# A new opening for a hybrid encoder block: 512-column value products, w_ada rows summed on VectorE, 4 KB loads

## The chip, the core and the metric

The kernel runs on one core of one Trainium2 chip. The metric is the device time of one execution in microseconds (us). The engines are TensorE (PE, matmuls; PEld is its weight load), VectorE (DVE), ScalarE (ACT), GpSimd (POOL) and SyncE (SP), which here issues nearly all DMAs. SBUF is the on-chip memory, PSUM the eight banks into which PE writes, HBM the main memory.

## The reference, cut to what matters

The block takes x (1024 positions by 1024 features, float32) and a conditioning vector c. Its opening is:

```python
ada = jax.nn.silu(c) @ w_ada[i] + b_ada[i]                 # 1024 -> 6 x 1024
shift1, scale1, gate1, shift2, scale2, gate2 = [...]       # ada in six parts
h = rmsnorm(x, g_mix[i]) * (1 + scale1) + shift1
proj = h @ w_in[i]
qa, ka, va, qb, kb, vb, ga, gb = jnp.split(proj, split_at, axis=-1)
oa = mixture_of_dilations(heads(qa), heads(ka), heads(va), rel_bias)
ob = neighbourhood_attention_2d(heads(qb), heads(kb), heads(vb), na_rpb[i])
```

va and vb have 512 columns each: 8 heads of 64 for branch A (dilated window attention) and for branch B (neighbourhood attention). After it come the two attentions, the gated merge with w_out, and a convolutional feed-forward layer with w_up and w_down. All of that stays as it is.

## The kernel before, in words

Every float32 operand of a large product is split into a high part (float32r, made by ACT) and the remainder (DVE or POOL: `split`, lines 54 to 56), and a product is three matmuls: high by high, high by low, low by high (`product`, lines 72 to 79). x lies in HBM as eight blocks k of 128 features by 1024 positions. The positions are worked in two halves of 512.

The opening is lines 110 to 369, most of it inside a block in which the order of every engine is written out by hand (`tc.manual_schedule`, line 288). It does this:

- It loads the first half of x in eight DMAs of 256 KB (`x_load`, 2 KB per partition), the first two chunks of w_ada, and halves of four weight tiles of w_in: q and k of head pair 0, and 256 columns of va.
- `square` (line 182) squares x on ACT and adds the squares on DVE; `square_sums`, `rstd_of` and `bcast` make the norm's factor in all partitions (PE sums, DVE, ACT, PE transposes).
- The w_ada chunks 0 to 3 hold shift1 and scale1, each for two of the eight blocks k. A chunk has eight rows of [128, 512]; each row is weighted with one column of silu(c) and all are added. In these four chunks three or four of the rows are weighted on ACT and added on POOL (`ada_rows_pool`, line 159), three or four on DVE (`ada_rows`, line 150, lines 155 and 157 of the profile), DVE joins the two (`ada_join`), and PE sums over the partitions (`ada_sums`, line 141). `piece_bias` (lines 263 and 265) then has the shift and scale of two blocks k.
- x is multiplied with the norm's factor on DVE or POOL (`scale_x`, line 206), and `modulate` (lines 212 to 215) makes the high and low part of h: ACT makes the high part from x, DVE the full value from x, DVE or POOL the difference.
- In four steps, each with two blocks k, PE then does the products of q and k of pair 0 with the first half (lines 77 to 79) and of 256 columns of va for four tiles of 128 positions (lines 247 to 249).
- Then the other 256 columns of va, the second half of x, and from line 484 on, left to a scheduler, the rest: query and key of pair 0 for the second half, va for the second half, vb in two halves of 256 columns, with w_ada chunks 4 to 11 (`ada_chunk`, line 168) in between. `va_chunks` and `vb_chunks` copy the values in HBM into the arrangements that the attentions read.

A chunk of w_ada is four DMAs of 512 KB, into tiles of several pools. Then comes `attend_dil` for pair 0: bias tables and values are loaded (lines 529 to 531, 449 to 452, `v_tile` at 473), the scores S (lines 557 and 558) go to a softmax (541, 542). Later pairs' query and key products and the gate products fill PE between the attention's matmuls.

Of the kernel before, what the change touches and what calls it, by code (L numbers as in the profile page):

```python
# [28 lines left out]
def hybrid_encoder(tc, xT, c, w_ada, small, w_in, p1_bias, p23_bias, na_bias, ln2_mult, ident, w_br, w_out,  # L29
# [55 lines left out]
    ps_g = tc.alloc_tile_pool(name="psg", bufs=2, space=PSUM)  # L85
    qkpool = tc.alloc_tile_pool(name="qk", bufs=3)
# [23 lines left out]
    early = tc.alloc_tile_pool(name="early", bufs=1, reuse_waits="tile")  # L110
    adapool = tc.alloc_tile_pool(name="ada", bufs=1, reuse_waits="tile")
    work = tc.alloc_tile_pool(name="start", bufs=2, reuse_waits="tile")
    ps_n = tc.alloc_tile_pool(name="psn", bufs=1, space=PSUM, reuse_waits="tile")
    ps_s = tc.alloc_tile_pool(name="psst", bufs=1, space=PSUM, reuse_waits="tile")

    slots = iter(range(1 << 20))

    def wada_tile(j):
        n = next(slots) if j < 4 else -1
        if n == 0:  # L120
            return qkpool.tile([128, 2, 512], FT, name="kl")
        if n > 0 and (n - 1) % 6 < 2:
            return early.tile([128, 2, 512], FT, name="wada", bufs=2)
        return adapool.tile([128, 2, 512], FT, name="wada", bufs=4)

    def ada_load(j):

        rows = []
        for t in range(0, KT, 2):
            wt = wada_tile(j)  # L130
            sp.dma_start(wt, w_ada[j][:, t:t + 2])
            rows += [wt[:, i] for i in range(2)]
        return rows

    def ada_sums(parts, pa=None, stop=True, n=4):

        first = pa is None
        pa = ps_s.tile([128, 4], FT, name="pada", bufs=1) if first else pa
        for i, (w, col) in enumerate(parts):
            for m in range(n):  # L140
                pe.matmul(pa[:, m:m + 1], w[:, m * 128:(m + 1) * 128], col, start=first and i + m == 0,
                          stop=stop and i == len(parts) - 1 and m == n - 1, skip_group_check=True)
        return pa

    def ada_bias(c0, pa, n=4):

        cc = slice(c0, c0 + n)
        dve.tensor_tensor(ada[:, cc], pa[:, :n], b_ada[:, cc], OP.add)

    def ada_rows(wt, ts, acc=None):  # L150

        for t in ts:
            if acc is None:
                acc = wt[t]
                dve.tensor_scalar(acc, acc, cs[:, t:t + 1], None, OP.mult)
            else:
                dve.scalar_tensor_tensor(acc, wt[t], cs[:, t:t + 1], acc, OP.mult, OP.add)  # L157

    def ada_rows_pool(wt, ts):
        for t in ts:  # L160
            act.activation(wt[t], wt[t], AF.Copy, scale=cs[:, t:t + 1])
        for t in ts[1:]:
            pool.tensor_tensor(wt[ts[0]], wt[ts[0]], wt[t], OP.add)

    def ada_join(wt, a, b):
        dve.tensor_tensor(wt[a], wt[a], wt[b], OP.add)

    def ada_chunk(j, wt):
        ada_rows(wt, range(KT))
        ada_bias(4 * j, ada_sums([(wt[0], ones)]))  # L170

    def x_load(hf, ks=range(KT)):
        x = []
        for k in ks:
            x.append(early.tile([128, 512], FT, name="xl", bufs=1) if hf + k == KT else h_tile(FT))
            sp.dma_start(x[-1], xT[k][:, halves[hf]])
        return x

    def sq_accs():
        return [early.tile([128, 512], FT, name="sq", bufs=2) for _ in range(2)]  # L180

    def square(x, accs, ks, e):
        for k in ks:
            acc = accs[k // 4]
            sq = early.tile([128, 512], FT, name="mt", bufs=4) if k % 4 else acc
            act.activation(sq, x[k], AF.Square)
            if k % 4:
                e.tensor_tensor(acc, acc, sq, OP.add)

    def square_sums(accs):  # L190
        pcol = ps_n.tile([128, KT], FT, name="pcol")
        add_sums(pcol, accs[0], True, False)
        add_sums(pcol, accs[1], False, True)
        return pcol

    def norm_bcast(pcol):
        return bcast(rstd_of(pcol, 4), ps_n, "pbc")

    def to_sbuf(pb):
        bc = early.tile([128, 512], FT, name="mt", bufs=4)  # L200
        act.activation(bc, pb, AF.Copy)
        return bc

    def scale_x(x, pb, bc, ks, e):
        for k in ks:
            e.tensor_tensor(x[k], x[k], pb if e is dve else bc, OP.mult)

    def modulate(x, hf, ks, lo_eng):
        for k in ks:
            a, b = am1[:, k:k + 1], ada[:, k:k + 1]  # L210
            hi, lo = h[hf, k] = h_tile(), h_tile()
            act.activation(hi, x[k], AF.Identity, bias=b, scale=a)
            t = early.tile([128, 512], FT, name="mt", bufs=4)
            dve.tensor_scalar(t, x[k], a, b, OP.mult, OP.add)
            lo_eng[k % 2].tensor_tensor(lo, t, f(hi), OP.subtract)  # L215

    def v_load(br, hv):
        return [w_load(w_in[(8, 20)[br] + 2 * hv + t]) for t in range(2)]

    v_pools = itertools.cycle((early, work))  # L220

    def v_tiles():
        p = next(v_pools)
        return tuple(p.tile([128, KT, 256], FR, name=n, bufs=1) for n in ("vwh", "vwl"))

    def v_split(raws, lo_eng, ks=slice(0, KT), w=None):
        hi, lo = w or v_tiles()
        for t in range(2):
            cc = slice(t * 128, t * 128 + 128)
            split(raws[t][:, ks], hi[:, ks, cc], lo[:, ks, cc], lo_eng[t])  # L230
        return hi, lo
# [8 lines left out]
    def v_product(st, w, p=None, ks=range(KT), fresh=True):  # L240

        hi, lo = w
        p = ps_s.tile([128, 512], FT, name="pv", bufs=3)[:, :256] if p is None else p
        sc = slice(st % 4 * 128, st % 4 * 128 + 128)
        for k in ks:
            hhi, hlo = (t[:, sc] for t in h[st // 4, k])
            pe.matmul(p, hhi, hi[:, k], start=fresh and k == 0, stop=False, skip_group_check=True)  # L247
            pe.matmul(p, hhi, lo[:, k], start=False, stop=False, skip_group_check=True)  # L248
            pe.matmul(p, hlo, hi[:, k], start=False, stop=k == KT - 1, skip_group_check=True)  # L249
        return p  # L250

    def v_out(br, hv, st, p):
        vs = work.tile([128, 256], FT, name="vs", bufs=3)
        act.activation(vs, p, AF.Copy)
        sp.dma_start((va_s, vb_c)[br][st * 128:st * 128 + 128, hv * 256:hv * 256 + 256], vs)
# [32 lines left out]
    with tc.manual_schedule(engines={e.engine for e in (sp, act, dve, pool, pe)}):  # L288
# [64 lines left out]
        for st in range(4):  # L353
            v_out(0, 0, st, pvs[0][st])
# [1007 lines left out]
```

## Time and profile before

| | |
|---|---|
| median of 3 runs | 1631.35 us (1630.24 to 4495.99) |
| profiled execution | 1631.86 us |
| its span in the profile | 1630.1 us |
| mean granted PE clock | 0.976 |
| PE busy | 1511.3 us (93%), 7884 matmuls |
| DVE / ACT / POOL busy | 1125.0 / 784.3 / 795.8 us |
| DMA | 196.87 MB, mean 121 GB/s |

The profile is of one execution. A row of a timeline has start and duration in us, engine, line, operation, out<-in, shape, how many in a row, and in brackets the idle time before it and what ended it. A row of stretches has the stretch, then busy us (and count) for PE, PEld, DVE, ACT and POOL, the granted PE clock, the busy share of the 16 DMA engines and GB/s. Starts of successive matmuls tell their pace better than their durations, since matmuls overlap.

### The profile page before, as it was taken

To read this page: it belongs to the slowest core of one execution; us is meant where nothing else is said; L and a number is where in the kernel's file an instruction comes from. 1 tells how busy PE (TensorE), PEld (TensorE's weight loads), DVE (VectorE), ACT (ScalarE), POOL (GpSimd) and SP (SyncE) were. 2 spreads that over 40 slices of the span, in tenths; PEclk is the share of its full clock that TensorE was granted. 3 is DMA by queue.
4 is the path that set the end of the run, shared out by engine and by line. 5 is a ranking of instruction groups with operands and counts; after the bars stand their busy time and mean duration, and the time that the engine had idled before them with its cause. 6 is when DMAs were issued, how large, how long until landed. Compare 5 with 4: busy or idle time off the path is not lost. (4 is left out here: it accounts for less than half of the span.)

```text
span 1630.1 us, 21921 instructions
## 1 busy us (share of the span) xinstructions
PE 1511.3 (93%) x7884; PEld 1285.9 (79%) x7884; DVE 1125.0 (69%) x1902; ACT 784.3 (48%) x1408; POOL 795.8 (49%) x493
## 2 busy tenths in 40 slices
PE   4898899999998999999999898999999997888998
PEld 3898888888897987887778677888888885766787
DVE  6886476676767766535625898876666669798875
ACT  4531276665766766543335454444444444333232
POOL 4442133243224443311156777676666666868622
PEclk9898999999999999999999999999999999999999
DMA  6749812222233452555534122232222232513222
GB/s 232 256 157 318 257 51 89 70 82 88 61 99 99 127 143 88 170 182 173 169 129 159 61 73 83 78 116 78 78 78 78 78 136 81 190 39 126 91 61 104
DMA packets 113525, 196.87 MB, mean 121 GB/s; under 512 B 40328, under 2 KB 61704, under 8 KB 113416
## 3 DMA queue, kind: packets, MB, share of 16 engines
q1 hardware_dynamic: 113144, 195.20, 36.6%
q8 instruction: 62, 1.02, 0.3%
q14 instruction: 47, 0.39, 0.1%
q10 hardware_dynamic: 272, 0.26, 0.0%
HBM read 158.73 MB, written 42.47 MB: 123 GB/s over the span
## 5 line engine op out<-in xcount | busy, mean ns | idle before, releaser
L56 POOL TENSOR_TENSOR wlo<-wraw,whi 128x1024 fp32r<-128x1024 f32 (+2 forms) x77 | 179.3, 2328 | 308.0 <-ACT whi L55 289.1
L77 PE MATMUL pj<-h,whi 128*128 128x512 f32 x448 | 181.8, 407 | 17.5 <-DVE kl L429 9.8
L78 PE MATMUL pj<-h,whi 128*128 128x512 f32 x448 | 180.2, 402 | 1.2 <-DVE h L215 1.2
L79 PE MATMUL pj<-h,wlo 128*128 128x512 f32 x448 | 179.8, 401 | 0.0
L56 POOL TENSOR_TENSOR wsl<-big,wsh 128x1024 fp32r<-128x1024 f32 (+1 forms) x45 | 110.2, 2451 | 61.6 <-ACT wsh L55 61.6
L1049 DVE SCALAR_TENSOR_TENSOR big<-wc,sm,big 128x256 f32<-128x256 f32 (+1 forms) x132 | 115.3, 921 | 17.2 <-ACT big L1043 17.2
L55 ACT ACTIVATE whi<-wraw 128x1024 fp32r<-128x1024 f32 (+2 forms) x81 | 81.0, 1000 | 77.2 <-PE pj L78 34.1
L77 PEld LDWEIGHTS pj<-h,whi 128*128 128x128 f32 x448 | 85.7, 192 | 35.6 <-issue 7.0
L78 PEld LDWEIGHTS pj<-h,whi 128*128 128x128 f32 x448 | 86.0, 192 | 16.8 <-DVE h L215 2.3
L79 PEld LDWEIGHTS pj<-h,wlo 128*128 128x128 f32 x448 | 85.7, 191 | 15.5
L542 ACT ACTIVATE P<-P,st 128x256 f32<-128x256 f32 x128 | 64.3, 503 | 47.2 <-DVE st L541 46.6
L541 DVE CUSTOM_DVE_ANT_0 P<-S,bias 128x256 f32<-128x256 f32 x128 | 52.1, 421 | 46.8 <-PE S L588 35.3
L474 POOL TENSOR_TENSOR vv<-vv 96x256 fp32r<-96x256 f32 (+2 forms) x32 | 40.9, 1287 | 85.3 <-ACT vv L473 62.5
L157 DVE SCALAR_TENSOR_TENSOR wada<-wada,cs 128x512 f32<-128x512 f32 x67 | 65.7, 980 | 19.4 <-DMA wada<-w_ada 17.6
L1049 DVE SCALAR_TENSOR_TENSOR big<-pj,sm,big 128x512 f32<-128x512 f32 x132 | 67.9, 563 | 16.1 <-ACT big L1043 16.1
L694 POOL TENSOR_SCALAR P<-P,stb 128x288 f32<-128x288 f32 (+1 forms) x32 | 40.2, 1257 | 79.1 <-DVE stb L691 62.1
L429 DVE SCALAR_TENSOR_TENSOR kl<-pj,ks 64x512 fp32r<-64x512 f32 x64 | 56.3, 880 | 30.3 <-ACT ks L427 29.7
L247 PE MATMUL pv<-vwh,h 128*128 128x256 f32 x256 | 74.4, 291 | 0.0
L56 POOL TENSOR_TENSOR wsl<-wraw,wsh 128x768 fp32r<-128x768 f32 (+1 forms) x23 | 53.4, 2323 | 42.9 <-ACT wsh L55 42.9
L249 PE MATMUL pv<-vwh,h 128*128 128x256 f32 x256 | 74.0, 289 | 0.0
L1043 ACT ACTIVATE big<-wc,sm 128x512 f32<-128x512 f32 x44 | 35.8, 815 | 79.0 <-DVE wc L877 45.8
L248 PE MATMUL pv<-vwl,h 128*128 128x256 f32 x256 | 73.4, 288 | 0.0
(360 smaller groups left out, 4948.4 us busy)
## 6 DMA issues: line engine op xcount, KB each, us to landing
wada<-w_ada SPq DMA_DIRECT2D x47, 512.0 KB, 5.3
wraw<-w_in SPq DMA_DIRECT2D x36, 512.0 KB, 4.0
big<-w_up SPq DMA_DIRECT2D x22, 512.0 KB, 5.5
wraw<-w_up SPq DMA_DIRECT2D x22, 512.0 KB, 3.6
as<-big SPq DMA_DIRECT2D x22, 512.0 KB, 3.0
big<-as SPq DMA_DIRECT2D x22, 512.0 KB, 7.7
wraw<-w_down SPq DMA_DIRECT2D x24, 384.0 KB, 3.6
gs<-gs SPq DMA_DIRECT2D x32, 256.0 KB, 2.0
```

The source lines that it names most:

```text
L55: act.activation(hi, raw, AF.Copy)
L56: lo_eng.tensor_tensor(lo, raw, f(hi), OP.subtract)
L77: pe.matmul(psum, whi[:, k0 + k], mhi, start=k == 0, stop=False)
L78: pe.matmul(psum, whi[:, k0 + k], mlo, start=False, stop=False)
L79: pe.matmul(psum, wlo[:, k0 + k], mhi, start=False, stop=k == n - 1)
L157: dve.scalar_tensor_tensor(acc, wt[t], cs[:, t:t + 1], acc, OP.mult, OP.add)
L247: pe.matmul(p, hhi, hi[:, k], start=fresh and k == 0, stop=False, skip_group_check=True)
L248: pe.matmul(p, hhi, lo[:, k], start=False, stop=False, skip_group_check=True)
L249: pe.matmul(p, hlo, hi[:, k], start=False, stop=k == KT - 1, skip_group_check=True)
L429: dve.scalar_tensor_tensor(ll[x], pp[a], 0.125, f(kh[a]), OP.mult, OP.subtract)
L542: act.activation(pp, pp, AF.Exp, bias=mi, scale=-1.0, accum_out=li)
L1049: dve.scalar_tensor_tensor(y[:, dst], src, wt, y[:, dst], OP.mult, OP.add)
```

## The change

The opening is written anew. Outside of it, two things change: `qk_tiles` no longer takes products begun in the opening, and x, whose layout in HBM is now [half][four pairs of k][128][2][512], is read back in the later stage with another index (256 KB as before).

- **Loads.** x comes in four DMAs of 512 KB for each half (4 KB per partition). The value weights have an array of their own, `w_v` [2][4][128][2][512], and are loaded as pairs of k for all 512 columns of a branch, 512 KB each. Neither q and k nor half tiles are loaded at the start.
- **w_ada.** All rows are added on DVE (`ada_rows`), into a small tile; of chunks 0 to 3, rows 6 and 7 are summed by PE directly with a column of silu(c). ACT and POOL have no part in it. The chunks go into whole 16 KB tiles (`t0`, `b1`, `b2`) that later or earlier hold split value weights, or into the four tiles of x: from chunk 4 on they alternate between `t0` and the x tiles.
- **modulate** takes x, scale and the norm's factor in one DVE instruction into a PSUM bank, ACT adds the shift and makes the high part from there, and DVE makes the low part from both. `scale_x` is gone.
- **Order.** PE does the values alone, 512 columns wide: branch A on the first half in four steps of two k, then 24 steps n of one k each: B on the first half, A on the second, B on the second. Between them stand the sums of w_ada chunks 4 to 11, one every second n. Query and key of pair 0 come behind all of it; their weights are split at n = 12. DVE splits no weights any more, POOL splits all.
- **Memory.** One PSUM pool of eight banks (five for values, two for stages, one for norms) is released before the query/key pool is made.

The core of the diff:

```diff
+    def ada_rows(rows, ts, acc=None):
+        for t in ts:
+            if acc is None:
+                acc = small_tile()
+                dve.tensor_scalar(acc, rows[t], cs[:, t:t + 1], None, OP.mult)
+            else:
+                dve.scalar_tensor_tensor(acc, rows[t], cs[:, t:t + 1], acc, OP.mult, OP.add)
+        return acc
...
+    def modulate(x, hf, ks, pb):
+        for k in ks:
+            hi, lo = h[hf, k] = h_tile(), h_tile()
+            t, b = stage(), ada[:, k:k + 1]
+            dve.scalar_tensor_tensor(t, x[k], am1[:, k:k + 1], pb, OP.mult, OP.mult)
+            act.activation(hi, t, AF.Identity, bias=b)
+            dve.scalar_tensor_tensor(lo, t, b, f(hi), OP.add, OP.subtract)
...
+    def v_split(raw, w, kp):
+        for i in range(2):
+            split(raw[:, i], w[0][:, 2 * kp + i], w[1][:, 2 * kp + i], pool)
+
+    def v_products(w, hf, k, banks, ts=range(4)):
+        hi, lo = w
+        for t in ts:
+            p = banks[t]
+            hhi, hlo = (x[:, t * 128:t * 128 + 128] for x in h[hf, k])
+            pe.matmul(p, hhi, hi[:, k], start=k == 0, stop=False, skip_group_check=True)
+            pe.matmul(p, hhi, lo[:, k], start=False, stop=False, skip_group_check=True)
+            pe.matmul(p, hlo, hi[:, k], start=False, stop=k == KT - 1, skip_group_check=True)
...
+        rows = {0: ada_load(0, "t0")}
+        raws = [v_load(0, 0)]
+        rows[1] = ada_load(1, "b1")
+        raws.append(v_load(0, 1))
+        rows[2] = ada_load(2, "b2")
+        raws += [v_load(0, kp) for kp in (2, 3)]
+        rows[3] = ada_load(3, "t0")
+        x.append(x_load(1))
+        vw = [(t16("a0"), t16("a1"))]
+        pcol = norm_sums(squares(x[0], (dve, dve)))
+        acc = ada_rows(rows[0], range(4))
+        r = rstd_of(pcol, 4)
+        pb = bcast(r, ps, "pc")
+        acc = ada_rows(rows[0], (4, 5), acc)
+        pa = ada_sums([(rows[0][t], cs[:, t:t + 1]) for t in (6, 7)] + [(acc, ones)])
+        v_split(raws[0], vw[0], 0)
+        banks = v_banks()
+        for q in range(4):
+            piece_bias(q, pa)
+            modulate(x[0], 0, range(2 * q, 2 * q + 2), pb)
+            v_products(vw[0], 0, 2 * q, banks)
             if q < 3:
+                v_split(raws[q + 1], vw[0], q + 1)
+                acc = ada_rows(rows[q + 1], range(6))
+                pa = ada_sums([(rows[q + 1][t], cs[:, t:t + 1]) for t in (6, 7)], stop=False)
+            v_products(vw[0], 0, 2 * q + 1, banks, (0, 1))
+            if q < 3:
+                ada_sums([(acc, ones)], pa)
+            v_products(vw[0], 0, 2 * q + 1, banks, (2, 3))
+        raws = [v_load(1, kp) for kp in range(4)]
+        vw.append((t16("b1"), t16("b2")))
+        rows = {4: ada_load(4, "t0"), 5: ada_load(5, None)}
+        pcol = norm_sums(squares(x[1], (dve, pool)))
+        v_split(raws[0], vw[1], 0)
+        r = rstd_of(pcol, 4)
+        v_split(raws[1], vw[1], 1)
...
+        for n in range(24):
+            g, k = divmod(n, 8)
+            br, hf = ((1, 0), (0, 1), (1, 1))[g]
+            if k == 0:
+                v_out(*old)
+                banks = v_banks()
+                old = br, hf, banks
+            if n == 17:
+                va_chunks(slice(0, 512))
+            v_products(vw[br], hf, k, banks)
+            if n == 1:
+                pb = bcast(r, ps, "pc")
+                modulate(x[1], 1, range(8), pb)
+            if n in (0, 1):
+                v_split(raws[n + 2], vw[1], n + 2)
+            if n in (5, 6):
+                qk_raw.append(w_load(w_in[4 * (n - 5)]))
+            i = n // 2 - 2
+            if n % 2 == 0 and i >= 0:
+                if i >= 2:
+                    pa = ada_sums([(accs[i - 2], ones)])
+                if i < 8:
+                    accs[i] = ada_rows(rows[4 + i], range(KT))
+                if i >= 2:
+                    ada_bias(4 * (i + 2), pa)
+                if i < 6:
+                    rows[6 + i] = ada_load(6 + i, (None, "t0")[i % 2 == 0])
+            if n == 12:
+                qk_w = [w_split(qk_raw[i], pool) for i in range(2)]
+        v_out(*old)
...
-        "xT": x[0][_POS].T.reshape(KT, 128, S),
+        "xT": x[0][_POS].T.reshape(4, 2, 128, 2, 512).transpose(3, 0, 2, 1, 4),
```

More of the change, by code (lines that the diff above doesn't have):

```diff
@@ L108, in h_tile @@
         return hpool.tile([128, 512], dtype, name="h", bufs=32)
[L110 to L143, printed above, removed]
@@ L217, in v_load @@
[L217 to L231, printed above, removed]
+    xpool = tc.alloc_tile_pool(name="xs", bufs=4, side="right", reuse_waits="tile")
```

296 lines of the change are left out of this document (97 added, 199 removed).

## The prediction, made before the changed kernel had run

> **What bounds the kernel now.** I read the profile page first, then the stretches of the first 230 us, then the timelines of TensorE (PE), VectorE (DVE), ScalarE (ACT), GpSimd (POOL) and SyncE (SP) there, and the order of instructions of both builds.
>
> ```profile
> span 1630.1 us, 21921 instructions
> PE   4898899999998999999999898999999997888998
> DMA  6749812222233452555534122232222232513222
> PE 32%; DVE 8%; issue 2%; DMA 0%; POOL 0%; ACT 0%; SPq 0%; DVEq 0%; ACTq 0%; POOLq 0%
> 0.00:230.00 230.00, 190.36 (x1260) 176.36 (x1261) 161.06 (x242) 95.90 (x182) 83.18 (x58) 0.94 0.66 221
> 300.00:1630.00 1330.00, 1251.49 (x6221) 1049.01 (x6219) 916.59 (x1523) 642.55 (x1115) 687.27 (x417) 0.98 0.33 106
> 140.00:180.00 40.00, 40.00 (x343) 40.00 (x341) 23.11 (x31) 6.43 (x15) 4.80 (x2) 1.00 0.96 319
> ```
>
> PE is busy 94% after 300 us, but 83% in the first 230 (the last two numbers of a stretch are the DMA share and GB/s). The change lies in that opening. (The chain that ended last does not reach back to it: it explains 42% of the span, from the end.) Behind it the two builds issue the same matmuls, from the second half of the attention on in the same order, so what the opening gains or loses is passed on to the end one for one. As landmark I take the restart of the attention scores, with all value products and the first 144 query/key products done:
>
> ```profile
> 27.63 0.79 PE L77 MATMUL pj<-h,whi 128*128 128x512 f32 x1 [3.83 <-ACT h L212]
> 29.80 0.63 PE L78 MATMUL pj<-h,whi 128*128 128x512 f32 x1
> 30.22 0.63 PE L79 MATMUL pj<-h,wlo 128*128 128x512 f32 x1
> 101.62 0.28 PE L247 MATMUL pv<-vwh,h 128*128 128x256 f32 x1
> 101.74 0.28 PE L248 MATMUL pv<-vwl,h 128*128 128x256 f32 x1
> 101.86 0.95 PE L141 MATMUL pada<-ones,wada 128*128 128x1 f32 x8
> 130.13 1.84 PE L141 MATMUL pada<-ones,wada 128*128 128x1 f32 x8 [7.08 <-issue]
> 193.25 0.39 PE L78 MATMUL pj<-h,whi 128*128 128x512 f32 x1
> 193.48 0.40 PE L79 MATMUL pj<-h,wlo 128*128 128x512 f32 x1
> 198.67 0.58 PE L557 MATMUL S<-ks,qs 128*128 128x256 f32 x1 [4.79 <-DVE st L541]
> ```
>
> From start to start: a 512-column matmul takes 0.23 us, 0.43 after an idle stretch; a 256-column one 0.12. A four-column w_ada sum (x8) takes 0.95, cold 1.84. By 198.67 PE has done 768 x 0.12 + 144 x 0.23 = 125 us of products; some 15 us are sums, and the rest is waiting and cold clock.
>
> **The change, part by part.**
>
> *Fewer, wider matmuls.* 768 x 0.12 = 92.2 become 384 x 0.23 = 88.3 us: -3.9 us of PE work, contained in the times below. They come in four groups of 96: branch A and branch B on the first half of x, then A and B on the second; a group has eight k, each of 12 matmuls (2.77 us). The query/key products stay 144, but none is interleaved with the value products any more.
>
> *The start.* Rows for this and the next part:
>
> ```profile
> 4.00:6.00 2.00, 0.00 (x0) 0.00 (x0) 0.00 (x0) 0.98 (x2) 0.00 (x0) 1.00 0.76 253
> 12.00:14.00 2.00, 1.05 (x6) 0.97 (x6) 0.95 (x2) 1.41 (x2) 0.00 (x0) 1.00 1.03 418
> L186 ACT ACTIVATE mt<-h x11: 615/629/630, 5.6 to 68.9; 128x512 f32<-128x512 f32 x11
> 15.68 1.12 PE L104 MATMUL pbc<-idt,rs 128*128 128x128 f32 x4 [0.71 <-DVE rs L98]
> 12.36 0.69 DVE L188 TENSOR_TENSOR sq<-sq,mt 128x512 f32<-128x512 f32 x1
> 26.38 0.15 DVE L263 TENSOR_TENSOR ada<-pada,sm 128x4 f32<-128x4 f32 x1
> 63.60 0.17 DVE L263 TENSOR_TENSOR ada<-pada,sm 128x4 f32<-128x4 f32 x1 [1.90 <-PE pada L141]
> 26.76 1.52 ACT L212 ACTIVATE h<-h,ada,am 128x512 fp32r<-128x512 f32 x2 [6.29 <-DVE am L265]
> 57.98 1.54 DVE L157 SCALAR_TENSOR_TENSOR wada<-wada,cs 128x512 f32<-128x512 f32 x2
> 29.98 6.72 DVE L157 SCALAR_TENSOR_TENSOR wada<-wada,cs 128x512 f32<-128x512 f32 x4
> 29.58 3.21 POOL L163 TENSOR_TENSOR wada<-wada 128x512 f32<-128x512 f32 x2 [3.68 <-ACT wada L161]
> 101.29 1.38 DVE L429 SCALAR_TENSOR_TENSOR kl<-pj,ks 64x512 fp32r<-64x512 f32 x2
> 17.83 1.31 ACT L55 ACTIVATE whi<-wraw 128x512 fp32r<-128x512 f32 x2
> ```
>
> x comes in four 512 KB loads instead of eight of 256 KB; the queue moves 253 GB/s at 4 to 6 us and 418 at 12 to 14, when 512 KB pieces of w_ada are in it, so I give it 0.9 us: the last square add ends at 12.1, not 13.05. Then DVE adds four w_ada rows (0.5 + 3 x 0.77) to 15.0, norm 0.6 and broadcast 1.1 to 16.8; PE's sums of rows 6 and 7 and of the accumulator are 24 cold matmuls instead of 16, at 1.84 per 8: 22.3. So the first bias (L263) stands at 22.2 instead of 26.38.
>
> *The four steps of the first half.* One step, from bias to bias: bias 0.4; then modulate, which now runs through PSUM as a chain, DVE 0.69, ACT 0.65, DVE 0.69 with three 0.05 us hand-overs, 2.1 us for each k and 4.2 for two (before, ACT and DVE both started from x: L212 0.72 each); then six rows on DVE, 0.5 + 5 x 0.77 = 4.4 us; then the sum 1.0. That is 10.0 us. POOL runs two weight splits of about 1.6 us under the rows, and the rows show what that does: four DVE adds took 6.72 us beside POOL, 1.7 each, against 0.77 alone. So 3.2 us of POOL costs DVE 1.7: 11.7 us for a step. [...] Three steps end at 22.2 + 35.1 = 57.3 (before: 63.60). PE needs some 8 us for a step and hides. The last 24 matmuls start 1.75 us later and take 5.5: 64.6.
>
> *From group to group.* PE now waits for x's second half: ACT's squares follow its last modulate (57.3 + 3.8 = 61.1) and take 8 x 0.63, POOL adds three of them behind (about 1.4 each) to 69.3, PE sums 1.0, and the first weight split of branch B ends at 70.7, on the same POOL queue. So PE idles some 5 us (64.6 to 70.7, with 1 us of sums) and is cold after it: 12 x 0.43 + 12 x 0.23 + broadcast 0.5 ends at 79.2.
>
> *A new wait.* ACT's last two weight splits stand behind all eight modulates of the second half in its order: 8 x 2.1 = 17 us from 79.2, then split 0.65 and POOL 1.4: 97.5. PE, after four more k of 2.77, is there at 90.3. It waits 7.2 us and restarts cold (4.7 for the first 12): 102.2. Queued behind it on PE are all later products.
>
> *The rest of the value products.* 17 k of 2.77 and eight sums of 0.95 end at 156.9. For that DVE must keep a pace of 6.5 us for each w_ada chunk: 0.5 + 7 x 0.77 + 0.2 = 6.1. POOL takes 4 us off it once:
>
> ```profile
> 126.35 2.34 POOL L56 TENSOR_TENSOR vwl<-wraw,vwh 128x1024 fp32r<-128x1024 f32 x1 [10.87 <-ACT vwh L55]
> 130.46 2.73 DVE L157 SCALAR_TENSOR_TENSOR wada<-wada,cs 128x512 f32<-128x512 f32 x1
> wada<-w_ada SPq DMA_DIRECT2D x47, 512.0 KB, 5.3
> 103.43 0.16 DVE L148 TENSOR_TENSOR ada<-pada,sm 128x4 f32<-128x4 f32 x1
> 193.11 0.16 DVE L148 TENSOR_TENSOR ada<-pada,sm 128x4 f32<-128x4 f32 x1 [4.29 <-PE pada L141]
> ```
>
> (two splits of 2.34, each of which freezes DVE about 2). And the loads: six chunks of 2.1 MB, four weight tiles of 0.52, one group's value stores (1.05) and half of the vb copies (1.84) are 17.6 MB that must land between 104 and 153 us, some 360 GB/s, against 319 at a share of 0.96 in the row of 140:180. At 335 they need 52.5 us, 3.5 more than there are; part of it is slack, and I take 1.5. The bounds are -2 and +20 (8.8 us for a chunk; before it was 89.7 / 7 = 12.8, paced by PE). V ends at 158.4.
>
> *Attention's start.* The first 72 query/key products end at 175.0. ACT's order then has the two value copies of head 0 and 1 between the copies of k, and these wait for loads that SP issues behind the last value stores:
>
> ```profile
> 189.43 0.59 SPq L738 DMA_DIRECT2D lnm<-ln_mult  x1
> 192.19 2.48 SPq L452 DMA_DIRECT2D vv<-vab  x2
> 196.92 1.69 SPq L452 DMA_DIRECT2D vv<-vab  x2
> 198.19 0.43 DVE L541 CUSTOM_DVE_ANT_0 P<-S,bias 128x256 f32<-128x256 f32 x1 [2.20 <-POOL bias L531]
> 199.65 1.04 ACT L473 ACTIVATE vv<-vv 128x1024 fp32r<-128x1024 f32 x1
> ```
>
> Before, SP took from 189.4 to 198.6 for that list. Begun at about 163 it ends at 173, landing 3 later, and with two copies of 1.04 the k copies end at 180.5: PE waits 5.5 us, about what it waits now (4.79). The other 72 products, 16.6 us, end at 197.1.
>
> **Sum.** 197.1 against 198.67 is -1.6 us. The profiled execution took 1631.86 us, 1.8 over its span and 0.5 over the median 1631.35: 1631.86 - 1.6, that is 1630 us. No change that can be told. Cost at nothing: the wider x layout read back later (256 KB loads of 2 KB runs as before, hidden in a stage with a DMA share of 0.33), the value stores (half as many, ACT is a quarter busy), and PSUM (eight banks, all taken by the new pool; the next pool waits for copies that end 2.4 us after the last product, while PE fills the two banks freed first).
>
> **Rivals.** *Faster, the waits melt.* If POOL's splits do not hold DVE up (three steps of 10.0: -5), the wait at 90.3 is half as long (-4, with -2 for the cold clock), the loads keep pace (-1.5) and the value copies are there in time (-5), the sum is -17.5 more: 1612. For it speaks that steps two to four of the first half wait for nothing but DVE; against it the row of 6.72 us. *Slower, the w_ada chunks set the pace.* There are two buffers; one is a single tile, which is refilled only when DVE has read all of it: 5.3 us to land from issue, four pieces and 14 vb copies in SP's order before chunk 10. If a chunk takes 8.8 us instead of 6.5, eight take 18 us longer: 1648. It decides from 6.7 us a chunk, where DVE's slack is gone. The share of 0.96 speaks for it; that before the same share held for 12.8 us a chunk with twice the small copies speaks against the full price. *The other clock.* PE idles four times for over 4 us. [...] If every step of the first half runs cold too, 12 x 0.20 = 2.4 us each, the last one alone reaches the end: 1633. *The change does not do what it says* (long runs do not bring x sooner): +0.9, within the forecast's range.
>
> **Chances.** The forecast (1620 to 1640, with the clock and the runs) 0.52; faster rival, 1605 to 1620, 0.20; slower rival, 1640 to 1658, 0.22; beyond these 0.06. The range from 1606 to 1656 leaves out little more than 0.15. Two per cent, about what a measurement of this kernel tells from no change, are 32.6 us: under 1598.7 lies only a sum of all melted waits and more, 0.03; over 1664.0 the slower rival with a slower first half, 0.06; within, 0.91.
>
> **What would show it.** In the profile after: the first bias add at about 22 us, the fourth at 57; an idle PE of 5 us near 65 to 70; one of 7 us near 90 to 97 that ends on POOL's last split; sums of w_ada every 6.5 us, not 8.8; value products over near 158; scores restarting near 180. I am wrong if the bias adds lie over 13 us apart, if the wait near 90 is not there, or if the time differs while the opening ends at the same place.

## The result, and the profile after

The changed kernel takes 1652.8 us (median of four, 1650.5 to 1654.9) against 1633.7 for the kernel before beside it (median of four): a ratio of 1.0121, with a 95% interval of 1.0096 to 1.0146. One of the four executions of the kernel before took 4496 us and is left out of the ratio. So the changed kernel is slower by 1.2%, some 20 us, where 1.6 us less were forecast. It is within the two per cent that were called no change, but the sign is clear, and the time lies outside the forecast's 1620 to 1640, in the range of the slower rival. Its profiled execution took 1650.49 us over a span of 1648.7, 18.6 us more span than before.

First the page of the changed kernel: the span, PE's and the DMA's busy tenths in 40 slices of 41 us, and the chain that ended last.

```profile
span 1648.7 us, 21067 instructions
PE   6787899999999999999999888999999997888998
DMA  9448512222224433545544213222222232513222
PE 63%; DVE 17%; DMA 6%; ACT 6%; issue 5%; POOL 2%; SPq 1%; DVEq 0%; ACTq 0%; POOLq 0%
```

PE's first five slices have 6 7 8 7 8, where the kernel before had 4 8 9 8 8; from slice 6 to 22 they are nearly alike. The DMA line has changed more: 9 4 4 8 5, with a hole in the second and third slices. The same stretches as before, and two more between them (length, then busy time of PE, PEld, DVE, ACT, POOL with instruction counts, granted clock, DMA share, GB/s):

```profile
0.00:230.00 230.00, 187.29 (x853) 154.59 (x854) 127.05 (x207) 71.82 (x131) 50.24 (x40) 0.91 0.60 216
300.00:1630.00 1330.00, 1257.78 (x6211) 1053.23 (x6210) 914.70 (x1522) 649.63 (x1128) 691.35 (x418) 0.98 0.33 105
140.00:180.00 40.00, 32.07 (x138) 26.42 (x137) 14.08 (x26) 3.58 (x6) 0.00 (x0) 0.83 0.75 261
70.00:105.00 35.00, 26.99 (x99) 20.98 (x99) 18.82 (x26) 12.02 (x22) 8.90 (x7) 0.80 0.08 30
105.00:155.00 50.00, 41.97 (x207) 34.60 (x205) 37.86 (x54) 5.68 (x8) 5.15 (x2) 0.94 0.94 337
```

From 140 to 180 us, where PE was busy without a break before, it is now busy 32 of 40 us, at a clock of 0.83. From 70 to 105 us the DMA engines stand nearly idle (0.08), and in the 50 us after that they are nearly full (0.94). The last score of the whole attention starts 18.1 us later than before (the first row is the kernel before, the second the changed one), so nearly all of the 18.6 us of span are lost by then:

```profile
672.90 0.29 PE L683 MATMUL S<-kl,qs 128*128 128x288 f32 x1
691.04 0.29 PE L617 MATMUL S<-kl,qs 128*128 128x288 f32 x1
```

The timeline shows where PE lost the time (start, duration, instruction, and in brackets the idle time before it with what ended it):

```profile
20.92 0.16 DVE L205 TENSOR_TENSOR ada<-st,sm 128x4 f32<-128x4 f32 x1 [4.70 <-PE st L140]
57.53 0.16 DVE L205 TENSOR_TENSOR ada<-st,sm 128x4 f32<-128x4 f32 x1 [1.23 <-PE st L140]
80.13 0.75 DVE L198 SCALAR_TENSOR_TENSOR st<-whi,am,pbc 128x512 f32<-128x512 f32 x1 [9.61 <-PE pbc L102]
97.37 0.80 PE L226 MATMUL pj<-b,h 128*128 128x512 f32 x1 [6.35 <-ACT b L55]
98.71 0.80 PE L227 MATMUL pj<-b,h 128*128 128x512 f32 x1 [0.55 <-POOL b L56]
155.31 1.83 PE L140 MATMUL st<-ones,mt 128*128 128x1 f32 x8 [7.93 <-DVE ada L167]
169.01 0.39 PE L77 MATMUL pj<-h,whi 128*128 128x512 f32 x1
191.33 0.77 PE L77 MATMUL pj<-h,whi 128*128 128x512 f32 x1 [3.67 <-DVE kl L389]
```

The opening runs as worked out up to the wait near 97 us. Then comes one of 7.93 us, ahead of the sum of w_ada chunk 10, where the sum held only 1.5 us for the loads, and the value products end at 169.0 us (the first query/key product follows them) instead of 158.4. VectorE and SyncE show what is behind it:

```profile
134.24 0.48 DVE L149 TENSOR_SCALAR mt<-x,cs 128x512 f32<-128x512 f32 x1
149.04 0.48 DVE L149 TENSOR_SCALAR mt<-t,cs 128x512 f32<-128x512 f32 x1 [8.21 <-DMA t<-w_ada]
128.14 1.84 SPq L434 DMA_DIRECT2D vb<-vbc  x2
131.98 11.51 SPq L434 DMA_DIRECT2D vb<-vbc  x14
143.59 2.09 SPq L162 DMA_DIRECT2D t<-w_ada  x4
173.62 1.86 SPq L434 DMA_DIRECT2D vb<-vbc  x3
175.58 0.53 SPq L672 DMA_DIRECT2D lnm<-ln_mult  x1
```

DVE stands still for 8.21 us until the first piece of chunk 10 has landed. The buffer `t0` was free from 134.2 us on, when DVE went over from chunk 8 to chunk 9, but SP issued the load of chunk 10 at 143.6. Ahead of it stood the vb copies: from branch B's values in DRAM to the layout that only the second half of the attention reads. Of the 32 copies, 16 can run once the first value group of branch B is stored; the scheduler put two of them ahead of chunk 9's last piece and 14 in a row ahead of chunk 10. Three of the other 16 stand, at 173.6, ahead of the attention's first loads.

### The profile page after: what moved, and what is told of

The parts are those of the page before. It is cut to its first block, busy times and chain, and to the rows that moved or that the text cites. A ratio compares the mean times of both kernels' runs of the same rounds, so it can differ in the third digit from the quotient of the medians.

```text
span 1648.7 us, 21067 instructions
## 1 busy us (share of the span) xinstructions
PE 1524.2 (92%) x7540; PEld 1277.6 (77%) x7540; DVE 1099.6 (67%) x1897; ACT 771.1 (47%) x1380; POOL 770.6 (47%) x481
## 4 chain that ended last, share of the span: by engine, by line
PE 63%; DVE 17%; DMA 6%; ACT 6%; issue 5%; POOL 2%; SPq 1%; DVEq 0%; ACTq 0%; POOLq 0%
PE pj L800 9%; PE pj L801 9%; PE pj L802 9%; PE pj L77 7%; PE pj L79 7%; PE pj L78 7%; DMA g<-gs 2%; DVE mt L151 2%; PE pj L362 2%; DVE big L984 2%; ACT ks L387 2%; PE O L650 1%; DVE kl L389 1%; DMA x<-w_ada 1%; DVE mlo L56 1%
## 5 line engine op out<-in xcount | busy, mean ns | idle before, releaser
L56 POOL TENSOR_TENSOR wlo<-wraw,whi 128x1024 fp32r<-128x1024 f32 (+1 forms) x77 | 182.0, 2364 | 296.1 <-ACT whi L55 284.2
L55 ACT ACTIVATE whi<-wraw 128x1024 fp32r<-128x1024 f32 (+1 forms) x79 | 80.7, 1021 | 99.1 <-PE pj L78 34.5
L55 ACT ACTIVATE wsh<-big 128x1024 fp32r<-128x1024 f32 (+1 forms) x45 | 44.8, 1000 | 47.6 <-POOL big L765 30.9
L387 ACT ACTIVATE ks<-pj 64x512 fp32r<-64x512 f32 x64 | 53.7, 839 | 16.1 <-DVE kl L389 8.4
L1010 ACT ACTIVATE big<-big 128x1024 f32<-128x1024 f32 x22 | 23.3, 1061 | 81.1 <-DVE big L984 81.1
L817 DVE TENSOR_TENSOR pj<-pj,wc 128x512 f32<-128x512 f32 x34 | 23.6, 695 | 53.2 <-PE pj L802 53.1
```

Source lines behind the costliest of these rows:

```text
L55: act.activation(hi, raw, AF.Copy)
L56: lo_eng.tensor_tensor(lo, raw, f(hi), OP.subtract)
L387: act.activation(kh[x], pp[a], AF.Copy, scale=0.125)
```

## The experiments

Each ratio is to the kernel before on the same chip, with its 95% interval (it lies within 0.0015 of the ratio of the medians), and "us" is that ratio less one, times 1631.6, the median of the kernel before beside the first experiments. An interval reaches 2 to 5 us to either side. "Values end" is the start of the first query/key product behind the value products in the profiled execution. Where lines are added, the line numbers move by a few; where the order is held by a list, all matmuls have the line of the helper that records them. A kernel that leaves out computation, run once, is not in the table.

| kernel | values end, us | ratio | us |
|---|---|---|---|
| changed | 169.0 | 1.0121 [1.0096, 1.0146] | +19.7 |
| vb copies late | 159.3 | 1.0014 [0.9991, 1.0038] | +2.3 |
| the same again | 157.3 | 1.0011 [0.9996, 1.0026] | +1.8 |
| only the later 16 vb copies late | 169.5 | 1.0078 [1.0051, 1.0104] | +12.7 |
| weight split first | 166.3 | 1.0125 [1.0099, 1.0151] | +20.4 |
| rows of chunk 4 early | 163.8 | 1.0097 [1.0071, 1.0122] | +15.8 |
| order of before, vb copies as changed | 171.0 | 1.0086 [1.0058, 1.0113] | +14.0 |
| order of before, vb copies late | 158.7 | 0.9983 [0.9968, 0.9999] | -2.8 |
| kernel before with the changed order | - | 1.0098 [1.0074, 1.0121] | +16.0 |
| vb copies late, third order | 157.9 | 1.0016 [1.0003, 1.0029] | +2.6 |
| three edits, new wait | 169.5 | 1.0084 [1.0063, 1.0105] | +13.7 |
| three edits, new wait, third order | 170.1 | 1.0077 [1.0058, 1.0097] | +12.6 |
| three edits, mended | 151.4 | 0.9995 [0.9978, 1.0013] | -0.8 |
| three edits, mended, order of before | 152.0 | 0.9954 [0.9937, 0.9972] | -7.5 |

**The vb copies late.** Each copy is put behind the last value load of the second head in SP's order. No matmul changes its place. The scheduler also moved two other instructions at the attention's start: ACT's value copy of the second head, which stood ahead of the second pair of k copies, now stands behind it, and one of POOL's bias multiplications stands later.

```
     d = sp.dma_start(vb_s[cb]..., vb_c[...])
+    issue_after(d.ins, va_last[1].ins)      # the last vv load of head 1
```

> The 32 vb copies are issued behind the second head's value loads instead of 14 of them ahead of the loads of w_ada chunks 10 and 11; the order of the matmuls is the one of the changed kernel throughout. Theory (the copies stand in front of the loads in SP's queue): PE's wait of 7.9 us before the sum of chunk 10 falls below 1.5 us, the cold stretch behind it goes, the value products end at 158 to 161 us instead of 169.2, and the span falls by 8 to 11 us, to 1638 to 1641 (median about 1643, still 0.6% slower than before). Rival (w_ada's bytes or DVE's rows set the pace, whatever stands in front): the wait stays over 4 us, the value products end after 165, the span falls by less than 4.

The expectation of the wait held and that of the time was too small: the wait is gone, and so is nearly the whole loss. From the profile of this kernel, SP's load of chunk 10 and of the attention's first table, DVE's first row of chunk 10, and PE's sum of chunk 10 (here L144):

```profile
135.67 1.75 SPq L166 DMA_DIRECT2D t<-w_ada  x4
141.99 0.48 DVE L153 TENSOR_SCALAR mt<-t,cs 128x512 f32<-128x512 f32 x1
149.28 0.95 PE L144 MATMUL st<-ones,mt 128*128 128x1 f32 x8
160.56 0.95 SPq L680 DMA_DIRECT2D lnm<-ln_mult  x1
```

The load is issued 7.9 us earlier, neither DVE nor PE waits for it, the sum runs at the warm 0.95 and not the cold 1.83, and the attention's loads begin at 160.6 instead of 175.6. Once issued, the load's first piece is there after 5.5 us in the changed kernel and after at most 6.3 here, so it is the later issue that the copies cost and not a slower load. The wait near 97 us is still there, and behind it PE waits for nothing until the value products end. The gain is 17 us where the value products gained 9.7. Two questions follow: what the rest is, and why the kernel is no faster than the one before (2 us slower, with zero inside the interval) when the value products end where they were forecast.

**The first 14 or the later ones.** Only the 16 copies that need the last value group (`r >= 2`) are moved; the first 16, the row of 14 among them, stay in front of chunk 10.

```
+    if r >= 2:
+        issue_after(d.ins, va_last[1].ins)
```

> Of the vb copies the 14 ahead of w_ada chunk 10 stay where they were; only the 16 that need the last value group are moved behind the second head's value loads, among them three that stood ahead of the loads of the attention's first bias and values. Theory (these three cost the attention's start 4 to 6 us, since SP waits in them for the last value stores to land): value products end at 169 as after the change, the first value loads are issued 4 to 6 us earlier, and the time is 1645 to 1649. Rival (the first 14 are the whole cause): within 2 us of the changed kernel, 1651 to 1655.

The value products end where they did (169.5), SP's last value stores and its next load stand as follows, and the time falls by 7 us:

```profile
168.28 3.33 SPq L241 DMA_DIRECT2D vbc<-mt  x4
171.71 0.41 SPq L681 DMA_DIRECT2D lnm<-ln_mult  x1
```

Without the three copies SP goes from the store to the table at once: 171.7 instead of 175.6. In the changed kernel SP waits in the first of the three until a value store has landed, as its waits say (line waited for, us in all, times, longest),

```profile
SPq L434 <- DMA vbc<-mt: 2.9, 1, 2.9
```

and issues the three in 1.9. So of 17.6 us the copies in front of chunk 10 cost some 10.6, about what the value products lost, and the others some 7, each number with about 6 us of play by the intervals. The two traces show less than 7 for the others: the loads begin 3.9 us earlier, the last of the first 144 query/key products starts 3.0 earlier (210.84 against 213.87), the attention's last score 0.6 and the end of the span 4.4. And the 10.6 are not the copies' place alone. These are ACT's second value copy and second pair of k copies, first with all copies late, then with the later 16 late:

```profile
175.47 1.20 ACT L391 ACTIVATE ks<-pj 64x512 fp32r<-64x512 f32 x2 [1.57 <-DVE kl L393]
176.57 1.04 ACT L431 ACTIVATE vv<-vv 128x1024 fp32r<-128x1024 f32 x1
```
```profile
185.57 1.06 ACT L431 ACTIVATE vv<-vv 128x1024 fp32r<-128x1024 f32 x1 [1.98 <-DMA vv<-vab]
186.66 1.20 ACT L391 ACTIVATE ks<-pj 64x512 fp32r<-64x512 f32 x2
```

Behind the second value copy the k copies come later, and PE then waits 2.82 us for k, against 1.86 and 0.83 in the two profiles with all copies late. So of the 10.6 some 1 to 2 us go with that order.

**Is it DVE's pace?** The rival was that DVE's rows, not the load, set the time. This kernel leaves out half of the rows of chunks 8 to 11.

```
-    accs[i] = ada_rows(rows[4 + i], range(KT))
+    accs[i] = ada_rows(rows[4 + i], range(KT) if i < 4 else (0, 3, 5, 7))
```

> Leaves out computation: for w_ada chunks 8 to 11 DVE sums four of the eight rows; loads, copies and sums on PE are as they were. Theory (the loads of chunk 10 are late): PE's wait before the sum of chunk 10 stays over 4 us and the value products end after 164 us. Rival (DVE's 6 us for a chunk is the pace): DVE saves 3 us a chunk, the wait goes, and the value products end at 157 to 160 us.

```profile
152.84 0.34 PE L140 MATMUL st<-ones,mt 128*128 128x1 f32 x1 [4.90 <-DVE ada L167]
```

With four rows fewer on each of these chunks, some 3 us at the 0.78 us that a row takes in the changed kernel, the wait is still 4.9 us, and the value products end only 3 us earlier, at 166.0: the load is late, not DVE. (One run, 1646.1 us.)

**The wait near 97 us.** The last weight split of branch B is emitted ahead of the second half's modulates.

```
-            if n == 1: pb = bcast(...); modulate(x[1], 1, range(8), pb)
             if n in (0, 1): v_split(raws[n + 2], vw[1], n + 2)
+            if n == 1: pb = bcast(...); modulate(x[1], 1, range(8), pb)
```

> The last weight split of branch B is emitted ahead of the second half's modulates instead of behind them. Theory (the wait is real but not on the path, since the w_ada chunks behind it are paced by DVE and the loads, which do not move): the waits of 6.4 and 0.6 us between 91 and 99 us go, a wait of 4 to 7 us for the sum of chunk 4 takes their place near 100, the wait for chunk 10 stays, the value products end within 2 us of 169.2 and the span changes by less than 3 us. Rival (the wait costs what it lasts, with its cold stretch): the value products end at 159 to 162 and the span falls by 7 to 10 us.

```profile
103.43 1.05 PE L140 MATMUL st<-ones,mt 128*128 128x1 f32 x8 [3.88 <-DVE mt L151]
153.62 0.55 PE L140 MATMUL st<-ones,mt 128*128 128x1 f32 x2 [7.74 <-DVE ada L167]
```

The wait is gone, one of 3.9 us for the sum of chunk 4 has taken its place, the one for chunk 10 is as long as it was, and the time has not changed (1.0125 against 1.0121). The value products end at 166.3, 2.8 us earlier, where at most 2 were expected. The wait that the prediction named was real and cost nothing in this kernel, for the late load behind it set the end. With the load on time it was not taken away alone.

**Rows earlier.** DVE idles 9.6 us ahead of the first modulate of the second half (row 80.13 above), with chunk 4 in `t0` and chunk 5 in the freed x buffers: both buffers are full, so nothing is loaded. Here chunk 4 is summed in that gap, and each later chunk moves up by one.

```
+            if n == 0:
+                accs[0] = ada_rows(rows[4], range(KT))
+                rows[6] = ada_load(6, "t0")
-            i = n // 2 - 2
+            i = n // 2 - 1
```

> The rows of w_ada chunk 4 are summed by DVE ahead of the second half's modulates, at 70 to 80 us, where DVE idles, and every later chunk and its load one slot earlier. Theory (the loads are late because the buffers stay full from 70 to 105 us while the queue idles): the load of chunk 6 is issued before 82 us instead of at 105, the wait for chunk 10 falls below 2 us, the value products end at 157 to 162 us, the span falls by 7 to 11 us; the wait near 91 stays or grows by up to 3 us. Rival (DVE needs 6.5 us for a chunk and POOL slows it by as much as is gained): the fourth to eighth sums still wait, the value products end after 165 and the span falls by less than 4.

```profile
145.40 0.80 PE L140 MATMUL st<-ones,mt 128*128 128x1 f32 x3 [3.27 <-DVE ada L167]
```

Chunk 6 is loaded from 80.5 us on, not from 105. The wait before chunk 10 shrinks to 3.3 us, over the 2 expected, while eight vb copies still stand ahead of that load. The value products end at 163.8, later than the 157 to 162 expected, and the time falls by 4 us instead of 7 to 11, between theory and rival: the idle DMA was part of the squeeze, and by itself the smaller part.

**All three edits.** The first version put the rows of chunks 4 and 5 ahead of the modulates and asked for the first sum at n = 6.

> Three edits of the opening together: vb copies behind the second head's value loads, the last weight split ahead of the second half's modulates, and the rows of w_ada chunks 4 and 5 ahead of them too, with the later sums one or two products further back; the matmuls of the attention keep the changed kernel's order. Theory (loads late, DVE idle from 70 to 80 us, and the wait near 91 were three separate losses, and once the chunks lead, the wait near 91 is on the path): value products end at 148 to 153 us, no wait over 2 us after 80, first 144 query/key products done at 187 to 192, and 8 to 10 us less than with the vb copies alone: 1623 to 1626. Rival (one of them only moves): value products end after 155 and the time stays at 1629 or more.

```profile
103.60 0.58 PE L144 MATMUL st<-ones,mt 128*128 128x1 f32 x2 [10.44 <-DVE h L204]
```

Here a new wait ate the gain: a sum is written to one of the two PSUM buffers "st" that the modulates also use, so it waits until DVE has read one of the last modulates, and these now come 8 us later (the first starts at 88.28 instead of 80.13). PE waits again at 140.3, 4.95 us for a sum. The values end at 169.5, and the theory fails on every count: the rival, that one loss only moves, holds. The next version puts only chunk 4 ahead, and asks for the sum of chunk 4 + i at n = 2i + 8:

> The three edits of the opening again, with the fault of the run of three edits mended: the rows of w_ada chunk 4 alone stand ahead of the second half's modulates, and the first sum on PE comes two products later, so that it does not ask for the PSUM buffer that the last modulate still holds. Theory: no wait of PE over 2.5 us between 80 us and the end of the value products, these end at 148 to 152 us, and 8 to 11 us less than with the vb copies alone: 1622 to 1626. Rival (the opening's end does not reach the end of the kernel, since the attention takes the longer the earlier it starts): value products at 148 to 152 but 1629 or more.

The values end at 151.4 us, 6 to 8 us earlier than with the vb copies alone. That is about what the prediction charged for the wait near 97 us, which is gone here together with the other losses. The gain in time is some 3 us: the rival's side of the expectation. Two waits of 2.97 us are left:

```profile
99.50 0.50 PE L230 MATMUL pj<-a,h 128*128 128x512 f32 x1 [2.97 <-ACT mt L240]
171.49 0.54 PE L81 MATMUL pj<-h,whi 128*128 128x512 f32 x1 [2.97 <-DVE kl L395]
```

The first is a PSUM bank of the third group, which waits for ACT's copies of the second behind the modulates. The second is the attention's start, where ACT's copies of k stand behind value copies that wait for their loads. It was 1.86 us in the first run with the vb copies late and 0.83 in the second: there the second value copy stood behind the k copies, here it is ahead of them again. From the end of the values to the last of the first 144 query/key products this kernel takes 41.5 us, those two 38.8 and 37.8, so some 3 of the 6 to 8 us are lost again there.

**The order of the attention.** The change alters the opening, and the scheduler then sorts the attention's matmuls anew; by operation, tiles and shape the two traces agree again only in the last 4247. So two kernels got a third order, by putting the value copies of the first two heads behind the copies of k:

```
     d = act.activation(vv[:m, cs_, 0:64], f(lo[:m, cs_]), AF.Copy)
+    if len(va_last) <= 2:
+        issue_after(d.ins, ks_last[0].ins)
```

> vb copies behind the second head's value loads, and the value copies of the first two heads behind the copies of k in ScalarE's order; the opening otherwise as changed. The value products end at 159.4 as with the vb copies alone. Theory (the order of the attention's matmuls costs 9 to 12 us against that of the kernel before): with another order 5 to 10 us under the 1633 of the vb copies alone. Rival: 1 to 3 us under it, for the 1.9 us wait at the attention's start.

> The edits of the run before, and the value copies of the first two heads behind the copies of k in ScalarE's order; the order of the attention's matmuls changes with it. Theory (the order in which the attention's matmuls stand after the change costs 9 to 12 us between 200 and 470 us, whatever the opening does): 5 to 12 us under the run before, 1613 to 1620. Rival (that stretch is no matter of the order): 1 to 3 us under it, for the wait at the attention's start alone.

Neither can be told from the kernel that it was made from: 1.0016 beside 1.0014, and 1.0077 beside 1.0084. The gains that were expected, the rival's 1 to 3 us among them, are not there. Another order, then, is not by itself a better one. The direct test holds the attention's matmuls in a given order, by a list taken from the other kernel. The orders of DVE, ACT and POOL then follow it: behind 200 us the traces differ in at most four instructions of each.

```
+    for a, b in zip(seq, seq[1:]):          # seq: the attention's matmuls in the order of the other kernel
+        issue_after(pe.log[first + b].ins, pe.log[first + a].ins)
```

> The vb copies behind the second head's value loads, as in the first run, and the attention's 2,600 matmuls held in the order in which the kernel before has them; nothing else is moved by hand. Theory (the other order in which the attention stands after the change costs about 10 us, whatever the opening does): 8 to 12 us under the vb copies alone, 1621 to 1625. Rival (the loss between 210 and 520 us is no matter of the order, since the run with the value copies behind the copies of k had a third order and the same loss): within 3 us of the vb copies alone, 1630 to 1636.

> The changed kernel with its vb copies where they were, and the attention's matmuls in the order of the kernel before. Theory (the traces are right, the order costs about 10 us between 210 and 520 us whatever stands before it): 1640 to 1645. Rival (the medians are right, the order is worth 3 to 5 us): 1647 to 1651.

> The kernel before, its opening untouched, with the attention's matmuls held in the order that they have after the change. Theory (the order costs about 10 us): 8 to 12 us over the kernel before. Rival: within 3 us of it.

> The first run again (its ten times spread over 17 us, and its profiled execution lay 5 us over its median): if the stretch from 210 to 520 us costs 11 to 13 us against the kernel before in this profile too, it belongs to the order; if it costs under 6, the first profile was an unlucky execution. The median should be 1631 to 1636.

The order of the kernel before is worth 14.0 against 19.7 with the vb copies as changed (5.7 us), -2.8 against 2.0 with them late (4.8), and, with the mended opening, -7.5 against -0.8 (6.7). By the intervals each of the three is good to 3.5 to 6 us, and the first alone could be nothing; the three together are clear of it. The theory had 8 to 12, the rivals under 3 and 3 to 5: the size lies between, nearer to the rivals, and by its time alone the first of these runs, 1630.1 us, would have been put down to its rival. The traces agree in sign and roughly in size. Their rows are the first product behind the values and the attention's last score:

```profile
170.96 0.39 PE L39 MATMUL pj<-h,whi 128*128 128x512 f32 x1
685.79 0.29 PE L39 MATMUL S<-kl,qs 128*128 128x288 f32 x1
```
```profile
157.29 0.39 PE L81 MATMUL pj<-h,whi 128*128 128x512 f32 x1
673.48 0.29 PE L625 MATMUL S<-kl,qs 128*128 128x288 f32 x1
```
```profile
158.68 0.39 PE L39 MATMUL pj<-h,whi 128*128 128x512 f32 x1
667.70 0.29 PE L39 MATMUL S<-kl,qs 128*128 128x288 f32 x1
```
```profile
151.41 0.39 PE L81 MATMUL pj<-h,whi 128*128 128x512 f32 x1
669.17 0.29 PE L627 MATMUL S<-kl,qs 128*128 128x288 f32 x1
```
```profile
151.98 0.39 PE L39 MATMUL pj<-h,whi 128*128 128x512 f32 x1
666.22 0.29 PE L39 MATMUL S<-kl,qs 128*128 128x288 f32 x1
```

The changed kernel (169.01 and 691.04 above) takes 522.0 us for this stretch and 514.8 in the order of before (first fence). With the vb copies late (second run) it is 516.2 and 509.0, and with the three edits mended 517.8 and 514.2. So the order is worth 7.2 us twice and 3.5 once. The same kernel's two profiled executions differ by 3.5 us in this stretch (519.7 in the first run), so that is as near as it goes. The repeated run had been asked whether the changed order costs 11 to 13 us: against the same kernel in the order of before it is 10.7 by the first profile and 7.2 by the second. The reverse test gives 16 us, more than its 8 to 12, and is no clean measure of the order: in the kernel before it also uncovers a wait that the products of the second pair had filled,

```profile
188.07 1.84 PE L39 MATMUL pada<-ones,wada 128*128 128x1 f32 x8 [7.07 <-issue]
```

so its 16 us are the order and a misfit to that opening together.

**Both.** The mended opening, the vb copies late, the order of before:

> The opening of the run before this one and the attention's matmuls in the order of the kernel before. Theory (two separate causes that add): 1611 to 1617. If only the opening counts 1622 to 1626, if only the order 1620 to 1625.

It takes 1625.7 us, less than both kernels: 0.46% under the one before (0.28 to 0.63). That is less than the sum that was expected, since each part is smaller than expected: from the 2 us lost with the vb copies late, 4.8 for the order and 2.8 for the opening would give -5.6, and it is -7.5. In its profile PE waits 3.3 us at 100 for a value copy and 3.5 us at 172.6 for k, the two waits named above.

## Why the prediction was wrong

- *Start and steps: right.* The first bias stands at 20.9 (22.2 was forecast), the fourth at 57.5 (57.3). The three steps take 12.2 us each, not 11.7, and the earlier start hides the difference. What the step charged for POOL is there: beside two splits on POOL (25.55 to 28.26 us, 2.71) DVE's six rows take 6.29 us (25.66 to 31.95), where rows without POOL beside them take 0.48 for the first and 0.78 for each other one (from 105.27 us), 4.4 for six. That is 1.9 more, where 1.7 were charged.
- *From group to group, and the new wait: right.* PE idles 2.05 and 1.11 us for x's second half, not 5. The first modulate of the second half starts at 80.1, after the broadcast forecast to end at 79.2; PE waits 6.9 us and goes on at 98.7, where 7.2 us and 97.5 were forecast (the terms as written add up to some 98). Its price, counted in full, was nothing in the changed kernel: without the wait it takes the same time, for a later load set the end. With the vb copies late no later wait hides it, and the values end where the count in full put them; there it was not taken away alone.
- *"For that DVE must keep a pace of 6.5 us" and the 1.5 us for the loads: this step failed.* DVE kept that pace: PE waits at most 0.33 us for a sum up to chunk 9. The bytes were summed as if they could land in any order, with half of the vb copies as 1.84 MB among 17.6. They came as one block ahead of one load. PE waited 7.93 us and then ran a sum (1.83 us) and 14 matmuls (0.43 us apart, at a granted clock of 0.50) cold. The values end 9.7 and 11.7 us later than in the two profiles with the copies out of the way, where 1.5 stood, and 10.6 later than forecast. With the copies late no wait of PE behind 100 us is left, so the other bytes, without the copies, cost nothing that shows. The bounds of this term, -2 and +20, held it; the range of the forecast did not.
- *The slower rival* named the copies in front of chunk 10, but had the wrong shape: 8.8 us for each chunk. The sums of chunks 4 to 9 start 6.4 to 6.9 us apart; one gap, the next, was lengthened to 14.5, mainly by SP's order and not by a rate. That its 18 us came near the measured 20 is luck: the values lost 10.6, and the rest was lost behind them.
- *Attention's start: the wait was right, what stands before it was not.* 5.5 us were forecast and 0.97 and 3.67 measured. But SP's list was to begin some 5 us after the values' end; it began 6.6 us after it, behind three copies that waited for a store, and by the times the later copies cost some 7 us in all, with 6 us of play.
- *"What the opening gains or loses is passed on to the end one for one": failed by some 5 us.* The same matmuls in the order of before take 4.8 to 6.7 us less. The prediction saw that the orders agree only from the attention's second half on, and costed the stretch before that at nothing.
- *The rest of the sum stands.* With the vb copies late and the order of before the kernel takes 2.8 us less than the one before (0.2 to 5.2), where 1.6 less were forecast, and its values end at 158.7, where 158.4 was forecast. That they meet so closely is partly luck: the 1.5 us that the loads did not cost made up for a restart behind the wait at 99.5, 2 us later than forecast, and the same kernel without the held order ends its values at 157.3 in one profile and 159.3 in another.

Still open is why the changed order is slower: a third order, with other waits, was no better, and no single wait was taken away to test it. Of the 7 us for the later copies 3.9 were seen at the loads. And the times of one kernel spread (1625 to 1642 in the ten runs of the first experiment), which its two traces do not explain.

## What to carry to other kernels

Read the queue of the engine that issues the loads in order and not in bytes: for each load that something waits for, ask what stands ahead of it that nobody needs yet, above all what a scheduler has hoisted there because its data were ready. A wait found in a timeline is worth its length only if what follows it isn't held by something later; take it away and see which wait comes next. And where a scheduler sorts what follows an edit, that order is part of the edit: compare it on every engine and not on one alone, hold it fixed to measure the rest, and price it as unknown and not as nothing.

## What the runs showed of the hardware

- Issuing takes time of its own: the 14 vb copies held SP for 11.5 us. A copy takes 0.60 us (median of 32), so some 8 us are issuing; in the rest SP waited for earlier loads to land (five waits, 3.8 us in all, none over 0.9). Chunk 10's first piece was there 5.5 us after SP issued it (143.6 to 149.0), and SP issued it 9.4 us after its buffer was free.
- In the changed kernel PE paid twice for its wait ahead of chunk 10: after 7.93 us idle (from 147.38 us) the sum of eight takes 1.83 us, against 0.95 where it did not wait, and the matmuls behind it start 0.43 us apart for some 6 us and 0.23 from then on. The granted clock shows it: 1.00 from 148 to 149 us, 0.68 from 149 to 150, 0.50 from 150 to 163, and 1.00 from 164 to 165.
- The same DMA engines carried 30 GB/s from 70 to 105 us and then 337 GB/s for 50 us. In the first stretch both w_ada buffers were full and DVE, their reader, was idle or busy with something else; the loads then crowded the second. Summing one chunk earlier moved a load from 105 to 80.5 us.
